# Down projection of a hybrid decoder layer: a second buffer of results for the first chunk, and the second sums scaled and added at the fifth product

## The chip, the cores and the metric

The kernel runs on one core of one Trainium2 chip. The metric is the time of one execution in device microseconds (us); shorter is better. The engines are named as the profile names them: PE (matmuls; PEld its weight loads), DVE (vector), ACT (scalar), POOL (GpSimd) and SP. SP and POOL issue nearly all transfers here.

## The reference

A decoder layer over 512 tokens and 16 meta tokens, width 2048: normalisation, one input projection, stick-breaking attention beside a gated short convolution, an output projection, and a SwiGLU feed-forward of width 5632. Only its last step is touched:

```python
n2 = _rmsnorm(h, g_ffn[l])
h = h + (jax.nn.silu(n2 @ w_gate[l]) * (n2 @ w_up[l])) @ w_down[l]
return h[:, N_META:]
```

The kernel holds everything transposed, as 16 output tiles of 128 features by 512 tokens. The normalisation's factor `r` is one number for each token, so it can be multiplied in after the product.

## The kernel before

**Numbers.** A float32 operand is split into a high part (`hi`, a cast, ACT, line 189) and a remainder (`lo`, a subtraction, DVE, line 190). A product of two tiles is three matmuls: hi by hi, hi by the activations' low part, lo by hi (lines 732, 733, 734).

**A pair of tiles by seven products.** `pair_product` computes two output tiles over two halves of the tokens as a 2x2 block product with Strassen's scheme in Winograd's form: seven block products instead of eight. In the down stage they run in the order x, z, x, z, x, y, x (first to seventh product), where x, y and z are PSUM banks with two buffers each. Seven sums of the activations, slots 0 to 6, are the moving operands. In between stand the evacuations: after the first product ACT copies x (p1, line 758), after the second z (p5, line 760), after the third x (u2, line 762); DVE forms `c2[:, 0]` after the fourth (line 764), `c2[:, 1]` after the fifth (line 768) and `c1[:, 0]` after the sixth (line 771); `c1[:, 1]` comes from the last x. So `c2` holds the "second sums", complete after the fifth product, and `c1` the "first sums", complete after the seventh. The fourth product adds onto z and so waits until line 760 has read it; the seventh adds onto x and waits for line 768.

**Chunks.** The inner dimension of the down projection, 22 blocks a half, goes in four chunks of 4, 6, 6 and 6 (`CHUNKS`). The first chunk is done with four output tiles at a time (`m=2`): 4 groups of seven products, each of 24 matmuls. They are called groups 0 to 3 here (`j` in the code). The other chunks have 8 pairs of two tiles each, seven products of 18 matmuls a pair.

**Results.** All sums lie in one buffer `d` of 4 x 512 numbers a partition. In the first chunk a group uses all of it: `c1` is `d[:, 0:2]`, `c2` is `d[:, 2:4]`, and since `sides` has no room for two tiles there, p5 is written to `c2[:, 1]` and u2 to `c2[:, 0]` by lines 760 and 762. In the later chunks pairs use the halves of `d` in turn. `scaled_sums` multiplies by r (`r_h`; line 1074 for c2, 1078 and 1079 for c1) and sends each tile to the output by a DMA that adds to what is there (`add_down`, line 1068, issued by POOL; "add" below).

**Loads.** Weights come by SP into `w_buf` as buffers get free. The activations of the chunk after come by POOL into ring places (`load_acts`, line 1040, two DMAs a slot, one each for the high and the low part; line 1033 is a small write that ties a load to the group before). The places of slots 5 and 6 of the second chunk are free only in group 3: slot 6's when the first three tiles of the pool `first` have been read. The names `fd1_6` and `ring1` in the rows below are slot 6 of the second chunk and its place.

**Order.** A scheduler places the instructions on the engines by its own estimates; each engine then runs its list in that order, and each waits only on semaphores. POOL's DMAs count on eight semaphores in turn (DMASW0 to 7).

Of the kernel before, what the change touches and what calls it, by code (L numbers as in the profile page):

```python
# [9 lines left out]
F32 = mybir.dt.float32  # L10
# [5 lines left out]
P = 128  # L16
D = 2048
SEQ = 512
# [8 lines left out]
T2 = SEQ // 2  # L27
# [6 lines left out]
def hybrid_layer(ctx: ExitStack, tc: tile.TileContext, xT, w_in, w_out, w_gu, w_down, vecs, out):  # L34
# [12 lines left out]
    def open_pool(name, bufs=1, **kw):  # L47
        return tc.alloc_tile_pool(name=name, bufs=bufs, reuse_waits="tile", **kw)
# [13 lines left out]
    def t512(cols=SEQ, tag="t", bufs=6):  # L62
        n_tmp[0] += 1
        pool = atmp if tag == "r" else tmp
        return pool.tile([P, cols], F32, tag=tag, bufs=bufs, name=f"tmp{n_tmp[0]}")
# [371 lines left out]
    def two(t):  # L437
        return t.rearrange("p (a b) -> p a b", a=2)
# [225 lines left out]
    def halves_of(cols):  # L664
        return t512(2 * CH, cols, 2)[:, : 2 * CH]

    for j in range(CONV_FIRST):
        if j == 0:
            after(2, lambda: form_blocks(7))
        c1, c2 = halves_of("e"), halves_of("e2")  # L670
# [45 lines left out]
    sides = cpool.tile([P, 3 * CH], F32, name="sides_c")  # L716
# [3 lines left out]
    def block_product(ps, act, start, m=1):  # L720

        hi, lo, n = next_w()
        w, n = ps.shape[-1] // m, n // m
        for j in range(m):
            p, skip = ps[:, j * w : (j + 1) * w], m > 1 or not start
            for k in range(n):  # L730
                kk = slice((j * n + k) * P, (j * n + k + 1) * P)
                pe.matmul(p, hi[:, kk], act(0, k), start=start and j == k == 0, stop=False, skip_group_check=skip)  # L732
                pe.matmul(p, hi[:, kk], act(1, k), start=False, stop=False, skip_group_check=skip)  # L733
                pe.matmul(p, lo[:, kk], act(0, k), start=False, stop=k == n - 1, skip_group_check=skip)  # L734

    def pair_product(acts, c1, c2, sides, m=1, fourth=None):

        i, cols = ents[used[0]][0], c1.shape[-1]
        w, first = cols // m, pairs[i][1]

        def bank(name):
            return xyz.tile([P, 512], F32, tag=name, name=f"{name}{i}")[:, :cols]

        def side(name):
            n = {"p1": 0, "p5": 1, "u2": 2}[name]
            if m == 1 or not n:
                return sides[:, n * w : n * w + cols]  # L750
            return c2[:, 2 - n]

        y, z, x = bank("y"), bank("z"), bank("x")
        p1, p5, u2 = side("p1"), side("p5"), side("u2")
        if first:
            block_product(y, acts[5], True, m)
        block_product(x, acts[0], True, m)
        sc.copy(p1, x)
        block_product(z, acts[1], True, m)
        sc.copy(p5, z)  # L760
        block_product(x, acts[2], False, m)
        sc.copy(u2, x)
        block_product(z, acts[3], False, m)
        ve.scalar_tensor_tensor(c2[:, 0], z, -1.0, u2, ALU.mult, ALU.subtract)
        if fourth:
            fourth()
        block_product(x, acts[4], False, m)
        ve.scalar_tensor_tensor(c2[:, 1], x, -1.0, p5, ALU.mult, ALU.subtract)  # L768
        if not first:
            block_product(y, acts[5], True, m)  # L770
        ve.tensor_tensor(c1[:, 0], y, p1, ALU.add)
        block_product(x, acts[6], False, m)
        return x

    def pair(acts):
        c1, c2 = halves_of("e"), halves_of("e2")
        x = pair_product(acts, two(c1), two(c2), sides)
        sc.copy(two(c1)[:, 1], x)
        return c1, c2

    for j in range(CONV_FIRST, HEADS, 2):
        ys = []
        for m in range(2):
            c1, c2 = pair(conv_acts)
# [16 lines left out]
        for m in range(2):  # L801
            s = t512(SEQ, "e", 2)[:, :SEQ] if j == HEADS - 2 else cpool.tile([P, SEQ], F32, tag="s", name=f"sq{j}_{m}")
# [45 lines left out]
    def pad(pool, n):  # L848
        pool.tile([P, n // 4], F32, name=f"pad_{pool.name}")

    acts = {}
# [33 lines left out]
    for i, j in enumerate(OUT_TILES):  # L885
# [32 lines left out]
        if i == KT - 1:  # L918
# [9 lines left out]
            sides = fp.tile([P, 3 * T2], F32, name="sides")  # L928
            rings_p = {0: open_pool("ring_0")}
            pad(rings_p[0], 32)  # L930
            rings, n_ring, ring = {}, [7], {}
# [3 lines left out]
            def new_places(i):  # L935
                p, m = groups[i]
                for n, t in enumerate(slots(rings_p[p], F32R, m, 6, f"ring{i}", tail=4 if i == 7 else 60, tag=f"ring{i}")):
                    ring[i + n] = t
# [31 lines left out]
    def act_of(t):  # L970
        return lambda part, k: t[:, part, k]
# [21 lines left out]
    at = [(c, k) for c, n in enumerate(CHUNKS) for k in range(n)]  # L993
# [32 lines left out]
    def load_acts(c, s, behind=None):  # L1026

        if c < len(CHUNKS):
            n = CHUNKS[c]
            if c:  # L1030
                rings[c, s] = ring_place()[:, :, :n]
                if behind is not None:
                    gp.tensor_scalar(rings[c, s][:, :, 0, 0], behind[:, :2], 1.0, 0.0, ALU.mult, ALU.add)
            elif s:
                rings[c, s] = slot(first, F32R, n, f"first{s}", f"first{s}")
            else:
                rings[c, s] = ring[0][:, :, :n]

            for part in range(2):
                gp.dma_start(rings[c, s][:, part], fd[c][s][:, part], max_dma_last_dim=3072)  # L1040

    for f in range(FT):
        g1 = apool.tile([P, 2, T2], F32, tag="c1", name=f"g{f}")
        u1 = apool.tile([P, 2, T2], F32, tag="c2", name=f"u{f}")
        x = pair_product(acts_of, g1, u1, sides, 1, None if f else h_scale)
# [7 lines left out]
    first = open_pool("ring_first", side="right")  # L1053
    with tc.high_priority(1 << 20):
        for s in range(1, 7):
            load_acts(0, s)
    pad(first, 11936)
    gate(FT - 1, g1, u1, x)
    apool.release()
    fpool_last.release()  # L1060
# [1 line left out]
    d = cpool.tile([P, 4, SEQ], F32, name="d")  # L1062
# [4 lines left out]
    def add_down(j, c):  # L1067
        gp.dma_start(two(out[j]), c, accum_op=ALU.add)  # L1068

    def scaled_sums(j, c1, c2, x, m):  # L1070

        for n in range(m):
            at = slice(n * T2, n * T2 + T2)
            ve.tensor_tensor(c2[:, :, at], c2[:, :, at], r_h, ALU.mult)  # L1074
            add_down(j + 2 * n + 1, c2[:, :, at])
        for n in range(m):
            at = slice(n * T2, n * T2 + T2)
            ve.tensor_tensor(c1[:, 0, at], c1[:, 0, at], r_h[:, 0], ALU.mult)
            ve.tensor_tensor(c1[:, 1, at], x[:, at], r_h[:, 1], ALU.mult)
            add_down(j + 2 * n, c1[:, :, at])  # L1080

    for j in range(KT // 4):
        for s in ((0, 1), (2, 3), (4,))[j - 1] if j else ():
            load_acts(1, s, last)
        c1, c2 = d[:, 0:2], d[:, 2:4]
        last = c2[:, 0]
        x = pair_product([act_of(rings[0, s]) for s in range(7)], c1, c2, sides, 2)
        if j == KT // 4 - 1:
            first.release()
            rings_p[1] = open_pool("ring_a", side="right")  # L1090
            for i in (1, 3, 4, 5):
                new_places(i)
            pad(rings_p[1], 160)
            for s in (5, 6):
                load_acts(1, s)
        scaled_sums(4 * j, c1, c2, x, 2)
    for c in range(1, len(CHUNKS)):
        end = c == len(CHUNKS) - 1
        for j in range(KT // 2):

            if 1 <= j <= 5:
                load_acts(c + 1, j - 1, last)
            c1, c2 = (two(d[:, j % 2 * 2 + m]) for m in range(2))
            last = c2[:, 0]
            last_pair = end and j == KT // 2 - 1
            if last_pair:
                h2 = slots(rings_p[1], F32, 1, 2, "h2", tag="ring4")[0].rearrange("p a k t -> p (a k) t")
                h2 = [h2[:, 2 * m : 2 * m + 2] for m in range(2)]
                for m in (1, 0):
                    nc.sync.dma_start(h2[m], two(out[2 * j + m]))  # L1110
            x = pair_product([act_of(rings[c, s]) for s in range(7)], c1, c2, sides)
            if j == KT // 2 - 1:
                for s in (5, 6):
                    load_acts(c + 1, s)
            if last_pair:
                ve.tensor_tensor(c2, c2, r_h, ALU.mult)
                ve.tensor_tensor(c2, c2, h2[1], ALU.add)
                nc.sync.dma_start(two(out[2 * j + 1]), c2)
                ve.tensor_tensor(c1[:, 0], c1[:, 0], r_h[:, 0], ALU.mult)
                ve.tensor_tensor(c1[:, 0], c1[:, 0], h2[0][:, 0], ALU.add)  # L1120
                ve.tensor_tensor(c1[:, 1], x, r_h[:, 1], ALU.mult)
                ve.tensor_tensor(c1[:, 1], c1[:, 1], h2[0][:, 1], ALU.add)
                nc.sync.dma_start(two(out[2 * j]), c1)
            else:
                scaled_sums(2 * j, c1, c2, x, 1)
    rings_p[2].release()
    cpool.release()
    rings_p[1].release()
# [59 lines left out]
```

## Time and profile before

| | us |
|---|---|
| median of 3 runs | 2090.63 (2089.04 to 2090.69) |
| the profiled execution | 2091.11 |
| its span, first to last instruction | 2087.8 |
| PE busy | 2046.0 (98%) |
| DVE busy | 1723.3 (83%) |
| ACT busy | 1046.5 (50%) |
| POOL busy | 414.9 (20%) |
| mean granted TensorE clock | 0.991 |

The times inside the trace are us from the span's start. A row of a timeline gives start and duration, engine, line, operation, output<-input, and in brackets how long the engine had waited and for whom. "PE busy" counts any time with a matmul under way; it does not say whether the matmuls follow each other at full pace. The down stage is the stretch from 1635.77 to the end.

### The profile page before, as it was taken

Reading aid. Unit: us, or ns where it says so; the run is one execution under the profiler, and the core shown is the slowest. Engines: PE = TensorE matmul, PEld = TensorE weight load, DVE = VectorE, ACT = ScalarE, POOL = GpSimd, SP = SyncE. Lnnn points to the kernel's source line nnn. Section 1 sums busy time; section 2 is a strip of 40 time slices with the busy share of each in tenths; the row PEclk is TensorE's granted clock in tenths of the full one; section 3 lists DMA queues with packets and bytes.
Section 4 is the critical chain, followed back from the end, with each engine's and each line's share of the span. In section 5 each row is a group of like instructions: output and inputs, shape, how many; then the busy total and the mean of one; then the engine's idle time right before and its main releaser. Section 6 shows DMA issues by size and latency. Waiting matters only on the chain.

```text
span 2087.8 us, 39731 instructions
## 1 busy us (share of the span) xinstructions
PE 2046.0 (98%) x16158; PEld 1979.0 (95%) x16158; DVE 1723.3 (83%) x2186; ACT 1046.5 (50%) x1511; POOL 414.9 (20%) x559
## 2 busy tenths in 40 slices
PE   8999999999999998999999999999999889999999
PEld 6999999999998888999999999999999889999999
DVE  7878877578877778998989989989899867888887
ACT  5666656444443435554555555545555433444443
POOL 3111111220015443111110111111101332223110
PEclk8999999999999999999999999999999989999999
DMA  6343334653356656556554555655555989989864
GB/s 205 107 152 118 121 123 133 219 154 106 103 205 186 183 177 217 153 175 175 163 162 149 169 154 148 173 155 162 164 150 172 300 239 237 262 233 252 242 155 86
DMA packets 161686, 362.21 MB, mean 173 GB/s; under 512 B 13456, under 2 KB 73360, under 8 KB 161504
## 3 DMA queue, kind: packets, MB, share of 16 engines
q1 hardware_dynamic: 78368, 225.80, 34.3%
q0 software_dynamic: 83136, 133.89, 24.4%
q8 instruction: 126, 2.06, 0.4%
q14 instruction: 56, 0.46, 0.1%
HBM read 278.76 MB, written 80.87 MB: 172 GB/s over the span
## 4 chain that ended last, share of the span: by engine, by line
PE 88%; DMA 3%; DVE 3%; issue 2%; ACT 1%; POOL 1%; SPq 0%; DVEq 0%; POOLq 0%; ACTq 0%
PE x L732 12%; PE x L734 12%; PE x L733 12%; PE z L732 6%; PE z L733 6%; PE z L734 6%; PE y L733 3%; PE y L732 3%; PE y L734 3%; PE po L829 3%; PE po L830 3%; PE po L831 3%; PE pv L276 1%; PE pv L278 1%; PE pv L280 1%
## 5 line engine op out<-in xcount | busy, mean ns | idle before, releaser
L189 ACT CAST s_buf<-w_buf 128x1024 fp32r<-128x1024 f32 (+2 forms) x665 | 659.4, 992 | 790.4 <-PE x L733 350.6
L190 DVE TENSOR_TENSOR s_buf<-w_buf,s_buf 128x1024 fp32r<-128x1024 f32 (+2 forms) x665 | 769.8, 1158 | 197.8 <-ACT s_buf L189 196.7
L733 PE MATMUL x<-f,s_buf 128*128 128x256 f32 x1408 | 388.3, 276 | 3.0 <-DMA f<-fx 1.8
L734 PE MATMUL x<-f,s_buf 128*128 128x256 f32 x1408 | 388.1, 276 | 3.0 <-DVE s_buf L190 3.0
L732 PE MATMUL x<-f,s_buf 128*128 128x256 f32 x1408 | 388.1, 276 | 0.2 <-ACT f L290 0.2
L198 DVE TENSOR_TENSOR w_buf<-w_buf 128x1024 f32<-128x1024 f32 (+1 forms) x243 | 278.5, 1146 | 19.0 <-DMA w_buf<-w_in 10.7
L733 PEld LDWEIGHTS x<-f,s_buf 128*128 128x128 f32 x1408 | 265.0, 188 | 3.4 <-DMA f<-fx 2.0
L734 PEld LDWEIGHTS x<-f,s_buf 128*128 128x128 f32 x1408 | 265.1, 188 | 3.2 <-DVE s_buf L190 3.2
L732 PEld LDWEIGHTS x<-f,s_buf 128*128 128x128 f32 x1408 | 265.0, 188 | 0.5 <-ACT f L290 0.4
L1002 POOL DMA_DIRECT2D fd<-s x147 | 103.9, 925 | 690.8 <-DVE s L291 689.2
L732 PE MATMUL z<-f,s_buf 128*128 128x256 f32 x704 | 193.6, 275 | 0.0
L733 PE MATMUL z<-f,s_buf 128*128 128x256 f32 x704 | 193.6, 275 | 0.0
L734 PE MATMUL z<-f,s_buf 128*128 128x256 f32 x704 | 193.6, 275 | 0.0
L732 PE MATMUL x<-ring,s_buf 128*128 128x256 f32 x608 | 168.1, 276 | 4.4 <-DVE d L768 4.4
L734 PE MATMUL x<-ring,s_buf 128*128 128x256 f32 x608 | 168.0, 276 | 1.0 <-DVE s_buf L190 1.0
L733 PE MATMUL x<-ring,s_buf 128*128 128x256 f32 x608 | 168.0, 276 | 0.0
L733 PEld LDWEIGHTS z<-f,s_buf 128*128 128x128 f32 x704 | 132.1, 188 | 0.1
L732 PEld LDWEIGHTS z<-f,s_buf 128*128 128x128 f32 x704 | 132.1, 188 | 0.0
L734 PEld LDWEIGHTS z<-f,s_buf 128*128 128x128 f32 x704 | 132.1, 188 | 0.0
L1068 POOL DMA_DIRECT2D out_T<-d x62 | 60.1, 990 | 326.6 <-DVE d L1074 273.8
L732 PEld LDWEIGHTS x<-ring,s_buf 128*128 128x128 f32 x608 | 114.8, 189 | 4.6 <-DVE d L768 4.6
L734 PEld LDWEIGHTS x<-ring,s_buf 128*128 128x128 f32 x608 | 114.9, 189 | 1.2 <-DVE s_buf L190 1.2
(380 smaller groups left out, 5310.2 us busy)
## 6 DMA issues: line engine op xcount, KB each, us to landing
w_buf<-w_gu SPq DMA_DIRECT2D x176, 512.0 KB, 3.4
w_buf<-w_in SPq DMA_DIRECT2D x92, 512.0 KB, 3.4
fd<-s POOLq DMA_DIRECT2D x147, 256.0 KB, 5.3
w_buf<-w_down SPq DMA_DIRECT2D x96, 384.0 KB, 4.9
ring<-fd POOLq DMA_DIRECT2D x42, 768.0 KB, 8.9
w_buf<-w_out SPq DMA_DIRECT2D x32, 512.0 KB, 3.5
out_T<-d POOLq DMA_DIRECT2D x62, 256.0 KB, 5.4
fc<-st SPq DMA_DIRECT2D x8, 1040.0 KB, 6.2
```

Of the source, the lines that this page charges most:

```text
L189: sc.copy(hi, src)
L190: ve.tensor_tensor(lo, src, hi.bitcast(F32), ALU.subtract)
L198: ve.tensor_tensor(sums[name], a, b, ALU.add)
L276: pe.matmul(ps, wh, ah[:, a:b], start=k == 0, stop=False)
L732: pe.matmul(p, hi[:, kk], act(0, k), start=start and j == k == 0, stop=False, skip_group_check=skip)
L733: pe.matmul(p, hi[:, kk], act(1, k), start=False, stop=False, skip_group_check=skip)
L734: pe.matmul(p, lo[:, kk], act(0, k), start=False, stop=k == n - 1, skip_group_check=skip)
L829: pe.matmul(ps, hi[:, kk], ah, start=k == order[0], stop=False)
L830: pe.matmul(ps, hi[:, kk], al, start=False, stop=False)
L831: pe.matmul(ps, lo[:, kk], ah, start=False, stop=k == order[-1])
L1002: gp.dma_start(fd[c][s][:, :, k], t[:, :, i])
L1068: gp.dma_start(two(out[j]), c, accum_op=ALU.add)
```

## The change

It has two parts. A second buffer `d2` of the same size is taken from the pool `first`, out of what was padding, and the first chunk's groups use `d` and `d2` in turn. And the work on the second sums (times r, add to the output) moves out of `scaled_sums` into `pair_product`, to a place behind line 768, as the function `second_sums`; `first_sums` keeps the rest. The very last pair is left as it was.

```diff
     def pair_product(...)
         block_product(x, acts[4], False, m)
         ve.scalar_tensor_tensor(c2[:, 1], x, -1.0, p5, ALU.mult, ALU.subtract)
+        if second:
+            second()
         if not first:
             block_product(y, acts[5], True, m)
...
-    pad(first, 11936)
+    d2 = first.tile([P, 4, SEQ], F32, name="d2")
+    pad(first, 11936 - 8192)
...
-    def scaled_sums(j, c1, c2, x, m):
-
-        for n in range(m):
-            at = slice(n * T2, n * T2 + T2)
+    def second_sums(j, c2, m):
+        for n, at in columns_of(m):
             ve.tensor_tensor(c2[:, :, at], c2[:, :, at], r_h, ALU.mult)
-            add_down(j + 2 * n + 1, c2[:, :, at])
+            add_down(j + n + 1, c2[:, :, at])
+    def first_sums(j, c1, x, m):
...
-        c1, c2 = d[:, 0:2], d[:, 2:4]
+        c1, c2 = (d, d2)[j % 2][:, 0:2], (d, d2)[j % 2][:, 2:4]
         last = c2[:, 0]
-        x = pair_product([act_of(rings[0, s]) for s in range(7)], c1, c2, sides, 2)
+        x = pair_product(
+            [act_of(rings[0, s]) for s in range(7)], c1, c2, sides, 2, None, lambda: second_sums(4 * j, c2, 2)
+        )
         if j == KT // 4 - 1:
             first.release()
...
             for s in (5, 6):
                 load_acts(1, s)
-        scaled_sums(4 * j, c1, c2, x, 2)
+        first_sums(4 * j, c1, x, 2)
```

The line numbers shift: 1068 becomes 1071 (the add), 1074 becomes 1079 (c2 times r), 1078 and 1079 become 1085 and 1086 (c1 times r), 771 becomes 773, 1033 and 1040 become 1035 and 1042.

What it moves lies in the first chunk and the first two pairs of the second; in the later chunks the scheduler had line 1074 behind line 768 already, and the lists are the same.

On ACT, in group 1 of the first chunk, there stood (`x54` and `z54` are that group's banks):

```order
L758 COPY sides_7920<-x54_17691 128x512 [waits DVE_49,PE_49]
L189 CAST s_buf_117<-w_buf_116 128x1024 [waits DVE_49,PE_49,Activation_49]
L760 COPY d_17468<-z54_17690 128x512 [waits DMASW7_49,DMASW1_49,PE_49]
L189 CAST s_buf_117<-w_buf_116 128x1024 [waits DMAHW2_49,DVE_49,PE_49]
L762 COPY d_17468<-x54_17691 128x512 [waits PE_49,Pool_49]
```

and now stands:

```order
L758 COPY sides_7920<-x54_17692 128x512 [waits DVE_49,PE_49]
L189 CAST s_buf_117<-w_buf_116 128x1024 [waits DVE_49,PE_49,Activation_49]
L760 COPY d2_17446<-z54_17691 128x512 [waits PE_49]
L189 CAST s_buf_117<-w_buf_116 128x1024 [waits DMAHW2_49,DVE_49,PE_49]
L762 COPY d2_17446<-x54_17692 128x512 [waits PE_49]
```

The copy of p5 no longer waits for the two adds of the group before (DMASW7 and DMASW1); in groups 2 and 3 it waits for those of two groups before.

On POOL, from the middle of group 2 to the end of group 3, there stood:

```order
L1040 DMA ring7_17473<-fd1_4_7965 128x2x768 [waits DMASW2_49]
L1068 DMA out_T<-d_17468 256x1x256 [waits DMASW3_49,DVE_49]
L1068 DMA out_T<-d_17468 256x1x256 [waits DMASW4_49,DVE_49]
L1040 DMA ring0_7925<-fd1_5_7966 128x2x768 [waits DMASW5_49,PE_49]
L1040 DMA ring0_7925<-fd1_5_7966 128x2x768 [waits DMASW6_49]
L1068 DMA out_T<-d_17468 256x1x256 [waits DMASW7_49,DVE_49]
L1040 DMA ring1_18321<-fd1_6_7967 128x2x768 [waits DMASW0_49,PE_49]
L1040 DMA ring1_18321<-fd1_6_7967 128x2x768 [waits DMASW1_49]
L1068 DMA out_T<-d_17468 256x1x256 [waits DMASW2_49,DVE_49]
L1068 DMA out_T<-d_17468 256x1x256 [waits DMASW3_49,DVE_49]
L1068 DMA out_T<-d_17468 256x1x256 [waits DMASW4_49,DVE_49]
```

and now stands:

```order
L1042 DMA ring7_17474<-fd1_4_7965 128x2x768 [waits DMASW2_49]
L1042 DMA ring0_7925<-fd1_5_7966 128x2x768 [waits DMASW3_49,PE_49]
L1071 DMA out_T<-d_17469 256x1x256 [waits DMASW4_49,DVE_49]
L1071 DMA out_T<-d_17469 256x1x256 [waits DMASW5_49,DVE_49]
L1042 DMA ring0_7925<-fd1_5_7966 128x2x768 [waits DMASW6_49]
L1071 DMA out_T<-d2_17446 256x1x256 [waits DMASW7_49,DVE_49]
L1071 DMA out_T<-d2_17446 256x1x256 [waits DMASW0_49,DVE_49]
L1071 DMA out_T<-d2_17446 256x1x256 [waits DMASW1_49,DVE_49]
L1071 DMA out_T<-d2_17446 256x1x256 [waits DMASW2_49,DVE_49]
L1042 DMA ring1_18326<-fd1_6_7967 128x2x768 [waits DMASW3_49,PE_49]
L1042 DMA ring1_18326<-fd1_6_7967 128x2x768 [waits DMASW4_49]
```

The two loads of slot 6 (`fd1_6`) stood behind the first of group 3's four adds; now they stand behind all four.

On PE, at the seventh product of the second chunk's first pair, which reads slot 6 (`x57` is its bank, `x58` that of the next pair's first product), there stood:

```order
L734 MATMUL y57_18340<-ring0_7925,s_buf_117 128x256
L732 MATMUL x57_18342<-ring1_18321,s_buf_117 128x256 [waits DMASW0_49,DVE_49]
L733 MATMUL x57_18342<-ring1_18321,s_buf_117 128x256 [waits DMASW1_49]
L734 MATMUL x57_18342<-ring1_18321,s_buf_117 128x256
L732 MATMUL x57_18342<-ring1_18321,s_buf_117 128x256
```

and now stands, after the first matmul of x57, which waits for slot 6's high part (DMASW3), and fourteen matmuls of x58:

```order
L734 MATMUL x58_18510<-ring7_17474,s_buf_117 128x256
L732 MATMUL x58_18510<-ring7_17474,s_buf_117 128x256
L733 MATMUL x58_18510<-ring7_17474,s_buf_117 128x256
L733 MATMUL x57_18343<-ring1_18326,s_buf_117 128x256 [waits DMASW4_49]
L734 MATMUL x57_18343<-ring1_18326,s_buf_117 128x256
```

So 17 matmuls of the next pair stand between the matmul that waits for the high part of slot 6 and the one that waits for its low part.

More of the change, by code (lines that the diff above doesn't have):

```diff
@@ L734, in block_product, with pair_product @@
                 pe.matmul(p, lo[:, kk], act(0, k), start=False, stop=k == n - 1, skip_group_check=skip)
-    def pair_product(acts, c1, c2, sides, m=1, fourth=None):
+    def pair_product(acts, c1, c2, sides, m=1, fourth=None, second=None):
         i, cols = ents[used[0]][0], c1.shape[-1]
@@ L1068, in add_down, with columns_of @@
         gp.dma_start(two(out[j]), c, accum_op=ALU.add)
-    def scaled_sums(j, c1, c2, x, m):
-        for n in range(m):
-            at = slice(n * T2, n * T2 + T2)
+    def columns_of(m):
+        return [(2 * n, slice(n * T2, n * T2 + T2)) for n in range(m)]
+    def second_sums(j, c2, m):
+        for n, at in columns_of(m):
             ve.tensor_tensor(c2[:, :, at], c2[:, :, at], r_h, ALU.mult)
-            add_down(j + 2 * n + 1, c2[:, :, at])
-        for n in range(m):
-            at = slice(n * T2, n * T2 + T2)
+            add_down(j + n + 1, c2[:, :, at])
+    def first_sums(j, c1, x, m):
+        for n, at in columns_of(m):
             ve.tensor_tensor(c1[:, 0, at], c1[:, 0, at], r_h[:, 0], ALU.mult)
             ve.tensor_tensor(c1[:, 1, at], x[:, at], r_h[:, 1], ALU.mult)
-            add_down(j + 2 * n, c1[:, :, at])
+            add_down(j + n, c1[:, :, at])
     for j in range(KT // 4):
@@ L1110, in hybrid_layer @@
                     nc.sync.dma_start(h2[m], two(out[2 * j + m]))
-            x = pair_product([act_of(rings[c, s]) for s in range(7)], c1, c2, sides)
+            x = pair_product(
+                [act_of(rings[c, s]) for s in range(7)], c1, c2, sides, 1, None,
+                None if last_pair else lambda: second_sums(2 * j, c2, 1),
+            )
             if j == KT // 2 - 1:
@@ L1124, in hybrid_layer @@
             else:
-                scaled_sums(2 * j, c1, c2, x, 1)
+                first_sums(2 * j, c1, x, 1)
     rings_p[2].release()
```

## The prediction

> **What bounds the kernel now.** I read the page first.
>
> ```profile
> span 2087.8 us, 39731 instructions
> PE 2046.0 (98%) x16158; PEld 1979.0 (95%) x16158; DVE 1723.3 (83%) x2186; ACT 1046.5 (50%) x1511; POOL 414.9 (20%) x559
> ```
>
> The matmuls fill the span, so a step matters only where PE waits for it or runs at a lower clock. Next, the view of waits, for the down stage alone (total us, count, longest).
>
> ```profile
> ACT d L760 <- DMA out_T<-d: 16.2, 3, 5.5
> PE z L732 <- ACT d L760: 13.0, 3, 4.4
> DVE d L764 <- DMA out_T<-d: 5.2, 1, 5.2
> PE x L732 <- DVE d L768: 4.7, 2, 4.4
> ```
>
> Three times ACT's copy of p5 waits for adds of the group before, which still read `d`, and three times PE's fourth product waits for that copy. Once DVE's line 764, in the second chunk's first pair, waits for an add, and PE's seventh product for line 768 behind it. Then PE's timeline.
>
> ```profile
> 1638.49 0.28 PE L732 MATMUL z<-first,s_buf 128*128 128x256 f32 x1
> 1641.21 0.28 PE L732 MATMUL x<-first,s_buf 128*128 128x256 f32 x1
> ...
> 1653.56 0.39 PE L734 MATMUL x<-ring,s_buf 128*128 128x256 f32 x1 [0.97 <-DVE s_buf L190]
> 1658.82 0.28 PE L732 MATMUL z<-first,s_buf 128*128 128x256 f32 x1
> 1668.79 0.58 PE L732 MATMUL z<-first,s_buf 128*128 128x256 f32 x1 [4.37 <-ACT d L760]
> 1673.87 0.28 PE L732 MATMUL x<-first,s_buf 128*128 128x256 f32 x1
> 1684.75 0.28 PE L732 MATMUL z<-first,s_buf 128*128 128x256 f32 x1
> 1711.40 0.28 PE L732 MATMUL z<-first,s_buf 128*128 128x256 f32 x1
> 1736.43 0.28 PE L732 MATMUL z<-ring,s_buf 128*128 128x256 f32 x1
> 1751.20 0.38 PE L732 MATMUL x<-ring,s_buf 128*128 128x256 f32 x1 [4.40 <-DVE d L768]
> 1757.03 0.28 PE L732 MATMUL z<-ring,s_buf 128*128 128x256 f32 x1
> 1771.31 0.28 PE L732 MATMUL z<-ring,s_buf 128*128 128x256 f32 x1
> ```
>
> The row at 1638.49 starts the second product of group 0, that at 1641.21 its third: 24 matmuls took 2.72 us, .1133 each. So a product of the first chunk costs 2.72 us and a group seven of them, 19.04. In the second chunk a product has 18 matmuls, 2.04 us, and a pair 14.28; the last two rows are 14.28 apart. The five other z rows begin the second products of groups 1 to 3 and of the second chunk's first two pairs. The fourth product of group 1 (1668.79) took 5.08 us instead of 2.72 after its wait; the last view, by windows (busy time, then clock, DMA share and GB/s), says why.
>
> ```profile
> 1620.90:1640.00 19.10, 19.10 (x171) 19.10 (x170) 15.98 (x19) 9.55 (x14) 7.61 (x11) 1.00 1.07 321
> 1640.00:1656.10 16.10, 15.13 (x133) 14.94 (x132) 15.75 (x19) 8.04 (x10) 1.40 (x2) 1.00 1.05 342
> 1656.10:1682.00 25.90, 21.53 (x170) 21.33 (x169) 16.29 (x19) 8.84 (x10) 9.58 (x9) 0.87 0.95 247
> 1668.79:1673.87 5.08, 5.08 (x25) 5.08 (x26) 1.22 (x1) 1.38 (x2) 0.00 (x0) 0.53 1.19 314
> 1682.00:1708.70 26.70, 22.28 (x171) 22.08 (x170) 17.59 (x22) 8.83 (x10) 8.88 (x10) 0.87 0.86 236
> 1708.70:1734.40 25.70, 21.23 (x171) 20.87 (x170) 17.41 (x23) 9.24 (x11) 10.31 (x12) 0.93 0.95 257
> ```
>
> The granted clock was 0.53 in that product: a wait of 4.4 us is paid a second time as matmuls at half pace.
>
> **The second buffer, in groups 1 to 3.** With `d` and `d2` in turn, line 760 waits for nothing in group 1, and in groups 2 and 3 for adds of two groups before. In group 2 those are group 0's, issued about a group (19 us) earlier; adds took 8.5 to 8.9 us to land (row below), so the wait goes. What PE wins is the distance between second products over 19.04: 1684.75 − 1658.82 = 25.93 gives 6.89; 1711.40 − 1684.75 = 26.65 gives 7.61; for group 3, 25.03 against six products of 2.72 and one of 2.04, 18.36, gives 6.67. Group 0's 20.33 holds no such wait: its 1.29 stays (.97 of it line 190). Group 3's may keep 0.3 of DVE lateness at line 768, which I leave in. Sum: 21.2 − 0.3 = 20.9.
>
> **The same in the second chunk's first pair.** `d` was last group 2's now, so line 764 finds it free, and line 768 comes in time: 1757.03 − 1736.43 = 20.60 against 14.28 gives 6.32. Gains together: 27.2 us.
>
> Of this 17.4 are the waits themselves (13.0 + 4.4), the rest is half clock. Another short wait shows that this second price has a threshold here:
>
> ```profile
> 806.69 0.38 PE L733 MATMUL x<-f,s_buf 128*128 128x256 f32 x1 [1.76 <-DMA f<-fx]
> 812.78 0.38 PE L734 MATMUL x<-f,s_buf 128*128 128x256 f32 x1 [2.96 <-DVE s_buf L190]
> 807.00:809.00 2.00, 2.00 (x20) 2.00 (x19) 0.00 (x0) 0.49 (x1) 1.35 (x2) 1.00 1.13 418
> 814.00:816.00 2.00, 2.00 (x11) 2.00 (x11) 1.97 (x2) 0.00 (x0) 0.00 (x0) 0.50 0.62 234
> ```
>
> After 1.76 us the clock stayed 1.00, after 2.96 it was 0.50. [...]
>
> **The second sums at the fifth product.** The instructions are the same in number and size: two multiplications by r in a group, two adds of c2, two of c1. They stand ahead of line 773 now instead of behind it, which makes line 773 later by at most one 0.69-us operation against a free next product; nothing on PE waits for it but the next evacuation of x. I take 0 in groups 0 to 3; the cover is DVE's room, 17.4 to 17.6 us of work for a group of 19.04. If it failed, DVE's lateness would cost the price of the second rival. In chunks two to four DVE's list is the same: 0.
>
> **The loads of slot 6, moved behind all adds of group 3.** This is the one new wait I expect. POOL before:
>
> ```profile
> 1738.13 1.12 POOL L1068 DMA_DIRECT2D out_T<-d  x1 [3.12 <-DVE d L1074]
> 1739.66 2.26 POOL L1068 DMA_DIRECT2D out_T<-d  x2 [0.41 <-DVE d L1079]
> ...
> L1068 POOL DMA_DIRECT2D out_T<-d x2: 1087/1098/1108, 1739.7 to 1740.8; - x2
> DMA to landing us min/median/max: 8.5/8.7/8.9
> ...
> L1040 POOL DMA_DIRECT2D ring<-fd x2: 1203/1208/1213, 1733.1 to 1733.8; - x2
> DMA to landing us min/median/max: 6.3/8.0/9.7
> ...
> L1040 POOL DMA_DIRECT2D ring<-fd x42: 737/772/2347, 1659.4 to 1960.4; - x42
> DMA to landing us min/median/max: 5.8/8.9/16.6
> ```
>
> The end of group 3 is E = 1736.43 − 2.04 = 1734.39. The loads of slot 6 went ahead of it, at 1733.1 and 1733.8, and landed 6.3 and 9.7 us later, 1739.4 and 1743.5: before the seventh product at 1751.20. The last adds went at 1739.66 and 1740.8, E + 5.3 and E + 6.4; they hang on DVE's work after line 768, which is the same in number. So the loads now go at about E + 7.1 and E + 7.8 (the queue's spacing in the rows above). Without other waits the seventh product starts at E + 6 x 2.04 = E + 12.24, 5.1 us after the first load's issue; the shortest of 42 loads took 5.8. So PE waits, by 0.7 to 11.5 us as the ends of that row have it (16.6 − 5.1). I take 7.9: the 6.3 of the same load, and about 1.6 for two adds (256 KB each) just ahead of it in the queue. The high and low parts (768 KB each) landed 1743.5 − 1739.4 = 4.1 us apart, so 512 KB are 2.7, of which some 1.1 us have passed while the adds are issued ahead. PE waits 2.8 us for the high part. The low part lands 4.1 later; 17 matmuls of the next pair (17 x .1133 = 1.9 at full pace) fill a part, and about 2.0 more is lost, as a wait or as half clock that fills it. Together +4.8, between 0.7 and 13.5 (11.5 + 2.0); a gain is excluded, since no matmul waited for slot 6 before.
>
> [...]
>
> **The sum.** 2091.11 (the profiled execution: span 2087.8 and 3.3 around it) − 27.2 + 4.8 = 2068.7. The median of the runs, 2090.63, lies 0.48 below that execution: 2068.2.
>
> **Rivals.**
>
> *No new wait at slot 6.* The loads go earlier than E + 7, since POOL is free before, or land in under 5 us. Then −27.5 − 0.48: 2063.1. For it: DVE's end after line 768 could come sooner with ACT no longer stalled. Against: no load under 5.8.
>
> *The DMA engines or DVE become the bound of the first chunk.* The groups would come in 19 us instead of 25 to 27, and move in that time what they move now. A group moves 247 GB/s x 25.90 = 6.40 MB, in 19.04 us 336 GB/s; the stretches at full clock moved 321 and 342 with a share of 1.05 to 1.07, so there is no room left above it. If weights come late, line 190 does, and PE with it, as in group 0 (1.29 us a group). Three groups so: +3.9, 2072. Its far end: groups as long as 20.33 plus one wait of 3 us and its half clock each (about 5 us, as between the 812.78 row and the clock's return), 2068.2 + 15 = 2083. Against: group 0 and the stretch ahead ran at full clock at that very rate.
>
> *Slower.* Slot 6, or a weight ahead of it, lands so late that the gain is eaten. The load would have to take 5.1 + 27 = 32 us from its issue, double the longest row, 16.6. Or each of the 28 products of the first chunk waits 1 us for its weights: the stage's weight loads landed within 11.9 us at most,
>
> ```profile
> DMA to landing us min/median/max: 2.9/4.9/11.9
> ```
>
> and would have to be later than the products they are issued ahead. From 28 x 1.0 = 28 us on it decides the sign; then 2091 and more.
>
> *No effect.* The adds of two groups before could still be under way, or the first wait be replaced by one of equal length at the same product (z's release by line 764): the waits stay, 2090.6. Against: 19 us of distance against 8.9 of landing.
>
> **How the numbers follow.** Forecast with the new wait (2064 to 2072): 0.59. No new wait (2062.5 to 2064): 0.15. DMA or DVE bound (2071 to 2083): 0.20. No effect: 0.03. Slower: 0.03. About 0.2%, 4.2 us, is what a measurement of this kernel can tell from no change. The first three cases all gain more than that: faster 0.59 + 0.15 + 0.20 = 0.94, same 0.03, slower 0.03. The low end is all the gain and no new wait, 2063.1 less 0.6 for the runs' own spread; the high end takes slot 6's load at 14 us (2091.11 − 27.2 − 0.48 + (14 − 5.1) + 2.0 = 2074.3) and the milder half of the DMA case: 2074.5. Left out are the other half of it, no effect and slower, 0.16.
>
> **What would show it.** Right: no wait of ACT's line 760 or DVE's line 764 for an add; second products of groups 1 to 3 19.0 to 20.4 us apart; clock 1.00 from 1660 to the end of group 3; one wait of 2 to 4 us at the seventh product of the second chunk's first pair, for the DMA into the ring, with a short stretch of half clock. Wrong: that wait over 8 us or missing, waits of PE for line 190 in every group, a fourth product that still waits for line 760.

## The result: 2070.75 us, and where the time went

| | us |
|---|---|
| before, median of 4 runs | 2090.66 (2089.04 to 2091.67) |
| after, median of 4 runs | 2070.75 (2066.04 to 2071.88) |
| ratio | 0.9887, 95% interval 0.9862 to 0.9912 |
| forecast | 2068.2, range 2062.5 to 2074.5 |
| the profiled execution after | 2071.88, span 2069.7 |

The page of the kernel after, the two lines that answer to those shown of before:

```profile
span 2069.7 us, 39728 instructions
PE 2038.4 (98%) x16158; PEld 1972.2 (95%) x16158; DVE 1724.3 (83%) x2186; ACT 1046.4 (51%) x1511; POOL 412.3 (20%) x559
```

Its shares for PE and DVE are those of before, 98% and 83%, and do not tell the two kernels apart; the waits of the down stage do. These are all of PE's:

```profile
PE x L732 <- DVE d L1085: 3.9, 1, 3.9
PE x L734 <- DVE s_buf L190: 0.7, 1, 0.7
PE x L732 <- DVE d L768: 0.3, 1, 0.3
```

The three waits for line 760 (13.0 us) and the 4.4-us wait for line 768 are gone, and one wait of 3.9 us is new. PE's timeline at the same products as before (the second products of groups 0 to 3 and of the second chunk's first two pairs, and the new wait), then the windows between them:

```profile
1640.58 0.28 PE L732 MATMUL z<-first,s_buf 128*128 128x256 f32 x1
1660.62 0.28 PE L732 MATMUL z<-first,s_buf 128*128 128x256 f32 x1
1679.66 0.28 PE L732 MATMUL z<-first,s_buf 128*128 128x256 f32 x1
1698.70 0.28 PE L732 MATMUL z<-first,s_buf 128*128 128x256 f32 x1
1717.62 0.28 PE L732 MATMUL z<-ring,s_buf 128*128 128x256 f32 x1
1731.92 0.77 PE L732 MATMUL x<-ring,s_buf 128*128 128x256 f32 x2 [3.93 <-DVE d L1085]
1738.95 0.28 PE L732 MATMUL z<-ring,s_buf 128*128 128x256 f32 x1
```

```profile
1640.58:1660.62 20.04, 19.34 (x170) 19.15 (x169) 19.45 (x23) 10.51 (x12) 4.38 (x4) 1.00 1.07 329
1660.62:1679.66 19.04, 19.04 (x170) 19.04 (x169) 16.33 (x19) 8.83 (x10) 9.19 (x14) 1.00 1.12 319
1679.66:1698.70 19.04, 19.04 (x170) 19.04 (x169) 17.18 (x21) 8.84 (x10) 8.59 (x11) 1.00 1.14 327
1698.70:1717.62 18.92, 18.64 (x164) 18.48 (x163) 17.03 (x23) 9.02 (x11) 6.89 (x8) 1.00 1.13 331
1717.62:1738.95 21.33, 17.40 (x129) 17.23 (x128) 13.38 (x21) 6.81 (x11) 6.67 (x8) 0.84 1.10 313
```

Groups 1 and 2 now take 19.04 us, the bare time of 168 matmuls, at clock 1.00; group 3 takes 18.92 against 18.36. The second chunk's first pair takes 21.33 against 14.28, at clock 0.84. The row at 1731.92 is put down to DVE's line 1085, which that matmul does not wait for; of its two semaphores, slot 6's load and line 768, the load came last. POOL's timeline, then the issues of that load by its line, with the time to landing:

```profile
1720.70 2.19 POOL L1071 DMA_DIRECT2D out_T<-d  x2 [4.53 <-DVE d L1086]
1722.37 2.01 POOL L1042 DMA_DIRECT2D ring<-fd  x2
```

```profile
L1042 POOL DMA_DIRECT2D ring<-fd x2: 1269/1276/1282, 1722.4 to 1723.1; - x2
DMA to landing us min/median/max: 9.4/10.6/11.9
```

1722.37 + 9.4 = 1731.8, and PE starts at 1731.92.

The stretch from group 0's second product to that of the second chunk's second pair, called **the stretch** below, took 1757.03 − 1638.49 = 118.54 before and 1738.95 − 1640.58 = 98.37 after: 20.2 less. The whole execution gained 2091.11 − 2071.88 = 19.2; the first chunk began 2.1 later in this execution (group 0's second product at 1640.58, not 1638.49), and the time around the span was 1.1 shorter (2.2, not 3.3). Behind the stretch both traces agree to 0.02 us. The two traced executions of the changed kernel, this one and the one below, are each the slowest of their four runs, so the stretch of the others may be shorter; no trace shows theirs.

### The profile page after: what moved, and what is told of

Same layout as the page of the kernel before. It is cut to its first block, busy times and chain, and to the rows that moved or that the text cites. A ratio compares the mean times of both kernels' runs of the same rounds, so it can differ in the third digit from the quotient of the medians.

```text
span 2069.7 us, 39728 instructions
## 1 busy us (share of the span) xinstructions
PE 2038.4 (98%) x16158; PEld 1972.2 (95%) x16158; DVE 1724.3 (83%) x2186; ACT 1046.4 (51%) x1511; POOL 412.3 (20%) x559
## 4 chain that ended last, share of the span: by engine, by line
PE 92%; DVE 3%; DMA 1%; ACT 1%; issue 1%; POOL 0%; SPq 0%; DVEq 0%; ACTq 0%; POOLq 0%
PE x L732 13%; PE x L734 13%; PE x L733 13%; PE z L732 6%; PE z L733 6%; PE z L734 6%; PE y L733 3%; PE y L732 3%; PE y L734 3%; PE po L831 3%; PE po L833 3%; PE po L832 3%; PE pv L276 1%; PE pv L278 1%; PE pv L280 1%; PE pk L278 1%
## 5 line engine op out<-in xcount | busy, mean ns | idle before, releaser
L198 DVE TENSOR_TENSOR w_buf<-w_buf 128x1024 f32<-128x1024 f32 (+1 forms) x243 | 278.6, 1146 | 18.9 <-DMA w_buf<-w_in 10.1
```

The lines of the kernel that those rows point to most:

```text
L198: ve.tensor_tensor(sums[name], a, b, ALU.add)
```

## The experiments

Runs of the changed kernel differ by up to 6 us, those of the kernel before by up to 12, and the traces reach the first chunk up to 3.7 us apart, though all kernels run the same list up to there (last section). So each experiment is read by its stretch in the trace as well as by its time. The last three rows belong to a second series of runs, with runs of the kernel before of their own, to which their ratios refer. E is the end of group 3, 2.04 us ahead of the second product of the second chunk's first pair.

| kernel | median us (range) | ratio to before, 95% | stretch us | groups 0 to 3 | first pair |
|---|---|---|---|---|---|
| before | 2091.09 (2085.25 to 2097.21); second series 2093.30 (2086.77 to 2095.25) | | 118.54 | 20.33, 25.93, 26.65, 25.03 | 20.60 |
| after, again | 2067.80 (2067.28 to 2070.72) | 0.9892 (0.9874 to 0.9911) | 97.32 | 20.05, 19.04, 19.04, 18.92 | 20.27 |
| first part alone | 2073.82 (2070.51 to 2074.63) | 0.9916 (0.9901 to 0.9931) | 101.72 | 20.04, 19.04, 19.04, 18.91 | 24.69 |
| second part alone | 2078.31 (2075.34 to 2081.03) | 0.9938 (0.9920 to 0.9955) | 111.19 | 21.01, 19.04, 25.60, 23.95 | 21.59 |
| buffers and halves exchanged | 2065.78 (2064.70 to 2069.09) | 0.9883 (0.9864 to 0.9901) | 93.09 | 20.37, 19.04, 19.04, 18.92 | 15.72 |
| buffers exchanged | 2072.29 (2071.67 to 2076.04) | 0.9905 (0.9886 to 0.9924) | 100.60 | 20.06, 19.04, 19.04, 18.91 | 23.55 |
| small adds | 2065.03, one run | | 93.84 | 20.04, 19.04, 19.04, 18.91 | 16.81 |
| second part, tied to c1 | 2075.04 (2072.99 to 2076.02) | 0.9913 (0.9898 to 0.9928) | 101.25 | 20.47, 19.04, 19.65, 20.93 | 21.16 |

**The changed kernel again.** No edit.

> The changed kernel once more, as the measure for the others of this call. Theory (the waits for adds are gone, one wait for slot 6 is new): 2066 to 2072 us; second products of groups 1 to 3 19.0 us apart, one wait of 3 to 5 us at the seventh product of the second chunk's first pair, whose two second products are 20 to 22 us apart instead of 14.28. Rival (the part of the 1.9-us spread that the profiled execution showed ahead of the down stage is no accident but belongs to the change): the stretch ahead of the first chunk is again about 2 us longer than in the kernel before.

```profile
1731.95 0.47 PE L732 MATMUL x<-ring,s_buf 128*128 128x256 f32 x2 [4.07 <-DMA ring<-fd]
1737.78 0.28 PE L732 MATMUL z<-ring,s_buf 128*128 128x256 f32 x1
```

PE's timeline: the wait came again, 4.07 us, and here the trace names the load. As the rival has it, the first chunk began late again (group 0's second product at 1640.46).

**First part alone.** The second sums are multiplied and added after the seventh product.

```diff
-        x = pair_product([...], c1, c2, sides, 2, None, lambda: second_sums(4 * j, c2, 2))
+        x = pair_product([...], c1, c2, sides, 2)
...
+        second_sums(4 * j, c2, 2)
         first_sums(4 * j, c1, x, 2)
```

> First part alone: d and d2 in turn in the first chunk, the second sums of a group times r and added after the seventh product as before. Theory (the second buffer carries the whole gain, and the move of the second sums is worth nothing beside it): the time of the changed kernel within 2 us; groups 19.0 apart, the loads of slot 6 again behind all four adds and a wait of 3 to 6 us for them. Rival (the early add is a part of the gain): slower than the changed kernel by 4 us or more, with waits of PE for line 760 or for line 768 left.

My theory fell here: the move of the second sums is worth 101.72 − 97.32 = 4.4 us beside the second buffer, or 3.4 against the first trace of the changed kernel. But it is not a wait for line 760 that it saves, as the rival thought; the groups take 19.04 without it. POOL's timeline, slot 6's landing, and PE's timeline at its wait, in this run:

```profile
1695.98 4.56 POOL L1035 TENSOR_SCALAR ring<-d 128x2 fp32r<-128x2 f32 x1
1700.85 0.75 POOL L1042 DMA_DIRECT2D ring<-fd  x1 [0.30 <-POOL ring L1035]
...
1720.84 2.01 POOL L1042 DMA_DIRECT2D ring<-fd  x2
```

```profile
L1042 POOL DMA_DIRECT2D ring<-fd x2: 1272/1280/1289, 1720.8 to 1721.6; - x2
DMA to landing us min/median/max: 13.3/13.9/14.5
```

```profile
1734.25 0.77 PE L732 MATMUL x<-ring,s_buf 128*128 128x256 f32 x2 [7.94 <-DMA ring<-fd]
```

The loads of slot 6 go as early as in the changed kernel, E + 6.9 against E + 6.8, and behind the same four adds, but the first lands 13.3 us after its issue instead of 9.4 and 9.6. What is late is the queue ahead of those adds. Slot 5's last load, by its line, in the first trace of the changed kernel and then in this run (the later of the two issues):

```profile
L1042 POOL DMA_DIRECT2D ring<-fd x1: 1733/1733/1733, 1704.1 to 1704.1; - x1
DMA to landing us min/median/max: 15.8/15.8/15.8
```

```profile
L1042 POOL DMA_DIRECT2D ring<-fd x2: 2328/2337/2346, 1704.2 to 1704.9; - x2
DMA to landing us min/median/max: 16.7/17.8/18.9
```

It landed at 1704.1 + 15.8 = 1719.9, E + 4.3, there, and at 1704.9 + 18.9 = 1723.8, E + 9.9, here. From slot 4's first load to slot 6's, POOL's transfers landed in the order of their issue in both traces, each 1.3 to 4.0 us behind the one ahead, so a late start of this queue is made good only in part. Slot 4's first load (1700.85) went at E − 13.1 here and at E − 18.6 in the changed kernel. Of these 5.5 us, 3.7 are line 1035's small write, which took 4.56 us instead of 0.83, and the rest is the add of c2 ahead of it, which goes later; 4.0 us of them are left when slot 6 lands. Why the write took longer is not shown.

**Second part alone.** One buffer d.

```diff
-        c1, c2 = (d, d2)[j % 2][:, 0:2], (d, d2)[j % 2][:, 2:4]
+        c1, c2 = d[:, 0:2], d[:, 2:4]
```

> Second part alone: one buffer d, the second sums times r and added at the fifth product. Theory (an add of c2 leaves about 0.5 us ahead of the group's end instead of 3.7 behind it and lands in 8 to 9.5, so line 760 is late by about 1.3 us a group, too little for half clock; the second chunk's first pair keeps its wait for the add of c1, 6.3 us with the half clock, and slot 6 is not late): 2091 - (20.9 - 3 x 1.3) = 2074 us, between 2070 and 2080. Rival 1 (when an add lands is set by the transfers' traffic, not by when it goes): 2088 to 2092, waits of 3 to 4 us left. Rival 2 (the move alone takes the waits wholly): 2069 to 2070.

PE's timeline at the fourth products of groups 2 and 3, and POOL's between groups 1 and 2:

```profile
1686.05 0.58 PE L732 MATMUL z<-first,s_buf 128*128 128x256 f32 x1 [3.51 <-ACT d L760]
1711.35 0.39 PE L732 MATMUL z<-first,s_buf 128*128 128x256 f32 x1 [3.22 <-ACT d L760]
```

```profile
1674.15 1.94 POOL L1035 TENSOR_SCALAR ring<-d 128x2 fp32r<-128x2 f32 x2
1675.25 1.51 POOL L1042 DMA_DIRECT2D ring<-fd  x1
1676.02 1.91 POOL L1071 DMA_DIRECT2D out_T<-d  x1
```

2078.31 lies in the expected range, but the waits are not as expected: none in group 1, over 3 us in groups 2 and 3. POOL's rows show why. Group 1 ends at 1676.93 − 2.72 = 1674.21. The second add of c2 goes 1.8 behind that instead of 0.5 ahead, since line 1035's two small writes and a load stand before it in POOL's list. In the second chunk's first pair the wait for line 768 stays, 4.58 us.

**Second part alone, with the loads tied to c1.** One word more.

```diff
-        last = c2[:, 0]
+        last = c1[:, 0]
```

> The second part alone (one buffer d), and the small write of line 1035 that ties a slot's load to the group before now reads c1 instead of c2, so that no load stands between a group's two adds of c2 in POOL's queue. Theory (in the run of the second part alone the second add went 1.5 to 1.8 us behind the group's end instead of 0.5 ahead, held up by that write and a load; it lands 8 to 9.4 later and line 760 waits for it): the waits of 3.5 and 3.2 us at line 760 shrink to 0.3 to 1.5, without half clock, so groups 2 and 3 take 19.3 to 20.5 us instead of 25.6 and 23.95; 100 to 104 us from the second product of group 0 to that of the second chunk's second pair, instead of 111.2. Rival (an add lands when the traffic lets it): waits over 2.5 us, 108 us or more.

PE's timeline at its three waits:

```profile
1684.05 0.39 PE L732 MATMUL z<-first,s_buf 128*128 128x256 f32 x1 [0.29 <-ACT d L760]
1705.12 0.39 PE L732 MATMUL z<-first,s_buf 128*128 128x256 f32 x1 [1.71 <-ACT d L760]
1733.43 0.58 PE L732 MATMUL x<-ring,s_buf 128*128 128x256 f32 x1 [4.33 <-DVE d L768]
```

With nothing between a group's two adds, the waits of 3.51 and 3.22 us fall to 0.29 and 1.71, and the stretch to 101.25, in the expected range (1.71 and group 3's 20.93 a little over theirs). So the wait for an add follows the add's place in POOL's list. Most of what d2 brings in the groups can be had without it: groups 1 to 3 take 59.6 us here, 77.6 before and 57.0 in the changed kernel.

**Buffers and halves exchanged.** d2 lies in the pool `first`, out of which slot 6's place comes. Here group 3 uses `d`, and the second chunk's pairs start with the half that held c2.

```diff
-        c1, c2 = (d, d2)[j % 2][:, 0:2], (d, d2)[j % 2][:, 2:4]
+        c1, c2 = (d2, d)[j % 2][:, 0:2], (d2, d)[j % 2][:, 2:4]
...
-            c1, c2 = (two(d[:, j % 2 * 2 + m]) for m in range(2))
+            c1, c2 = (two(d[:, (j + 1) % 2 * 2 + m]) for m in range(2))
```

> The changed kernel with d2 for groups 0 and 2 and d for groups 1 and 3, so that d2, which lies in the pool whose release frees slot 6's place, is not used by group 3; and the second chunk's pairs begin with the half of d that held c2. The loads of slot 6 then stand behind two adds instead of four. Theory (their place in POOL's queue makes them late): they go about 0.5 us behind group 3's end, 11.7 ahead of their use, so the wait is gone or under 1 us: 2063 us, 5 to 8 below the changed kernel. Rival (transfers are slow there because the DMA engines are full, wherever the loads stand): the wait moves to a weight or to line 764 and the time stays within 2 us of the changed kernel.

Slot 6's loads by POOL's timeline and by their line, and PE's timeline at its wait:

```profile
1713.82 1.99 POOL L1042 DMA_DIRECT2D ring<-fd  x2
```

```profile
L1042 POOL DMA_DIRECT2D ring<-fd x2: 1250/1256/1263, 1713.8 to 1714.5; - x2
DMA to landing us min/median/max: 10.9/11.8/12.8
```

```profile
1727.39 0.38 PE L733 MATMUL x<-ring,s_buf 128*128 128x256 f32 x1 [1.14 <-DMA ring<-fd]
```

The loads go at E + 0.1, with two adds ahead of them, not four, and land no sooner after their issue than in the changed kernel (10.9 and 12.8). What counts is the place in the queue, two adds further ahead: the first lands at E + 11.0 instead of E + 16.2. PE waits 1.14 us for the low part, and the stretch is 93.09, 4.2 and 5.3 below the two traces of the changed kernel. It is the best version here by its trace; by the times, where 5 to 8 us less were expected, it can't be told from the changed kernel (2065.78 and 2067.80, and the intervals overlap).

**Buffers exchanged alone.** The same without the second line of the diff.

> As the version with exchanged buffers and halves, but the second chunk's pairs begin with the half of d that held c1, as in the kernel before. Theory (the 6.3 us of the second chunk's first pair hang on line 764 finding its half of d still under an add): the adds of c1 go at about 5.1 and 6.2 us behind group 3's end and land near 14, line 764 needs the place at 8.2; the seventh product waits 3.5 to 4.5 us for line 768 and half clock follows: the pair's second products 20 to 21.6 apart, 97 to 99.5 us from the second product of group 0 to that of the second chunk's second pair (93.1 with the halves exchanged, 97.3 in the changed kernel). Rival (the wait in that pair was slot 6 all along): 93 to 94 us, since slot 6's loads stand behind two adds here too.

DVE's wait in the view of waits, group 3's adds of c1 by their line, and PE's timeline:

```profile
DVE d L764 <- DMA out_T<-d: 6.9, 1, 6.9
```

```profile
L1071 POOL DMA_DIRECT2D out_T<-d x2: 1104/1113/1122, 1719.4 to 1720.5; - x2
...
DMA to landing us min/median/max: 10.7/10.8/10.9
```

```profile
1732.75 0.58 PE L732 MATMUL x<-ring,s_buf 128*128 128x256 f32 x1 [6.13 <-DVE d L768]
```

The wait of the kernel before is back, though both parts of slot 6 had landed by 1728.8, 4.0 us before the wait ended: it hung on line 764 and the half of `d`, not on slot 6. It is larger than expected, 6.13 us instead of 3.5 to 4.5, because the adds land 10.7 to 10.9 us after their issue, not 8.5 to 8.9. 1.5 MB of slot 6 now go 5 us ahead of them in the same queue, and the first of the adds landed 1.3 us behind the last of it.

**Small adds.** The two adds of c1 of group 3 send 16 of 128 partitions; the rest of those two tiles is not added.

```diff
-    def add_down(j, c):
-        gp.dma_start(two(out[j]), c, accum_op=ALU.add)
+    def add_down(j, c, rows=P):
+        gp.dma_start(two(out[j])[:rows], c[:rows], accum_op=ALU.add)
...
-            add_down(j + n, c1[:, :, at])
+            add_down(j + n, c1[:, :, at], 16 if m == 2 and j == KT - 4 else P)
```

> The changed kernel, in which the two adds of c1 of group 3, right ahead of slot 6's loads in POOL's queue, send only 16 of 128 partitions (32 KB instead of 256 KB each); the rest of those two tiles is left out of the output. Number and place of the transfers are the same. Theory (the bytes just ahead of a load in its queue are what makes it land in 9.5 us instead of 6.3): the load lands 6 to 7.5 us after its issue, PE's wait is 0.3 to 2 us, and no half clock follows; the pair's second products 14.6 to 16.5 apart. Rival (a load of 768 KB takes that long because the weights and loads as a whole fill the DMA engines): landing 9 to 10, wait 3.5 to 4.5, 20 to 21.5 apart.

Slot 6's loads by POOL's timeline and by their line, and PE's timeline at its waits:

```profile
1718.90 1.99 POOL L1042 DMA_DIRECT2D ring<-fd  x2
```

```profile
DMA to landing us min/median/max: 7.0/8.3/9.6
```

```profile
1726.04 0.47 PE L732 MATMUL x<-ring,s_buf 128*128 128x256 f32 x2 [1.03 <-DMA ring<-fd]
1729.26 0.39 PE L733 MATMUL x<-ring,s_buf 128*128 128x256 f32 x1 [0.91 <-DMA ring<-fd]
```

The load lands in 7.0 us instead of 9.6, and PE's wait falls from 4.07 to 1.03 and 0.91; 0.5 us of that is the earlier issue (E + 6.3 against E + 6.8). The bytes of the adds just ahead make the load late; 448 KB less of them are 2.6 us. In the queue, the two small adds had landed 1.1 us after the adds of c2 ahead of them, the full ones 3.7 us after. The pair's 16.81 is 0.2 over the expected range.

## Why the prediction was right, point by point

**The waits that go.** Right. Groups 1 to 3 gained 6.89 + 7.61 + (25.03 − 18.92) = 20.6 us, where 20.9 was forecast, after the 0.3 that I left in group 3; line 768 kept 0.28 there. Lines 760 and 764 wait for no add any more. The landing of 8.5 to 8.9 us that stands behind this was read from two late adds; others of the kernel before took up to 14.7 (issued at 1662.86), still less than the 19 us between groups. The loss in the second chunk's first pair was line 764's: with that wait gone and 1.14 us of slot 6's left the pair takes 15.72 (halves exchanged), with line 764's wait back 23.55 (buffers exchanged).

**The new wait.** Right in place and cause, too small in size: 4.8 was forecast; the pair lost 21.33 − 14.28 = 7.05 us in the profiled execution and 5.99 in the other. Three terms: the issue came at E + 6.8 (E + 7.1 forecast); the high part landed 9.4 us later, not 7.9; and the half clock behind the wait cost 7.05 − 3.93 = 3.1, and 1.9 in the other execution, where 2.0 stood. The step that was mis-sized is "some 1.1 us have passed": I priced the two adds by a load's rate, 2.7 us for 512 KB, and took off what moves during the issue. The runs put the delay that the two adds leave at 2.6 us for 448 KB. And more was under way than the two: when the load went at 1722.37, the second add of c2 and both adds of c1 had yet to land, which they did 2.1, 3.5 and 5.7 us later, and the load followed 3.7 us behind the last. In the kernel before, one add was ahead of the same load; it landed 3.3 us after the load's issue and the load 3.0 behind it, which is the 6.3 that the sum started from. The low part brought no wait of its own; the 17 matmuls of the next pair, at half pace, covered it.

**The second sums cost 0.** The cover held: DVE had 16.3 to 17.2 us of work in 19.04, and line 773 held up nothing on PE (ACT's line 758 once, by 0.4 us). That they also gain, 3.4 to 4.4 us, I had not seen; that gain was inside the forecast's number only because the order of the changed kernel was read as it is.

**The sum.** In the profiled execution the stretch gained 20.2 instead of 27.2 − 4.8 = 22.4, the other time 21.2. The medians, 2070.75 and 2067.80, lie around the forecast of 2068.2; their difference is of the size of the spread.

**The rivals.** No new wait: not so, 3.93 us. DMA engines or DVE as the bound: not so; groups 1 to 3 ran at clock 1.00 with a DMA share of 1.12 to 1.14 at 319 to 331 GB/s, above group 0's 1.07, and no wait for line 190. So there was room above the share of 1.05 to 1.07 that the prediction held to be full. No effect, slower: not so.

## What to carry to other kernels

A second buffer takes away a wait, but see what its memory was lent from: here it made a load that comes out of the same pool go behind four adds, and about a quarter of the 27 us was paid back. Price a transfer by its place in its issuer's list and by everything ahead of it that has yet to land, not by its own size alone: here an add of 256 KB landed 1.3 to 3.2 us behind the transfer ahead of it in the changed kernel's traces. Count a wait together with the slow stretch behind it, where one follows: here 3.1 us were lost at half clock behind a wait of 3.93.

## What the runs showed of the hardware

**In these traces the loss at half clock did not follow the length of the wait.** Behind waits of 3.93 to 7.94 us in the second chunk's first pair, the next 36 matmuls, 4.08 us at full pace, took between 5.83 (wait 4.07: 1737.78 − 1731.95) and 7.06 us (wait 6.13): 1.8 to 3.0 us lost, 2.3 behind the longest (1740.63 − 1734.25 = 6.38 in the first part alone). In the changed kernel alone it was 3.0 in the first trace and 1.8 in the second. The stretches at half clock in the down stage of the kernel before, and those between them (busy times, then clock, DMA share and GB/s):

```profile
1666.78:1673.61 6.83, 4.82 (x22) 4.82 (x23) 1.22 (x1) 2.02 (x3) 0.00 (x0) 0.50 1.18 339
1673.61:1694.09 20.48, 16.74 (x148) 16.54 (x146) 15.95 (x19) 6.82 (x7) 8.88 (x10) 1.00 0.82 229
1694.09:1700.91 6.82, 6.14 (x28) 6.14 (x29) 1.78 (x2) 2.85 (x4) 0.00 (x0) 0.50 1.18 320
1700.91:1721.39 20.48, 16.27 (x142) 16.07 (x142) 15.49 (x19) 6.80 (x9) 8.35 (x9) 1.00 0.76 202
1721.39:1724.81 3.42, 3.42 (x17) 3.42 (x18) 1.23 (x1) 1.21 (x2) 0.00 (x0) 0.50 1.13 320
1724.81:1752.11 27.30, 22.64 (x196) 22.28 (x195) 19.98 (x28) 10.25 (x14) 5.88 (x6) 1.00 0.93 248
1752.11:1755.53 3.42, 3.42 (x18) 3.42 (x17) 3.42 (x6) 0.84 (x1) 2.32 (x4) 0.50 0.46 62
```

All seven last 3.41 us or 2, 6 or 8 times that, to 0.01. The one stretch at half clock in the down stage of the changed kernel, in its first trace and then in its second:

```profile
1731.14:1737.96 6.82, 6.04 (x28) 6.07 (x29) 0.67 (x2) 0.84 (x1) 0.99 (x2) 0.50 1.14 368
```

```profile
1732.75:1736.15 3.40, 3.40 (x19) 3.40 (x18) 0.00 (x0) 0.61 (x1) 0.00 (x0) 0.50 1.14 344
```

In the first, 6.0 us of it lay behind the wait's end at 1731.92, and 3.0 were lost; in the second all 3.4 lay behind the wait's end at 1731.95, and 1.8 were lost: about half of it both times. After waits of 1.71 us and less in the down stage the matmuls kept their pace (behind the 1.71, in the run tied to c1, the clock was 1.00 from 1705.10 to 1709.00).

**Of two waits of nearly one length, one had half clock behind it.** In the run of the second part alone PE waited 2.31 us up to 805.69 and 2.37 up to 811.20, ahead of the down stage. Its trace in windows of 3.41 us, laid from the start of the stretch at half clock, with PE's busy time first:

```profile
801.06:804.47 3.41, 2.32 (x20) 2.06 (x18) 3.12 (x3) 1.53 (x3) 1.27 (x2) 1.00 1.07 397
804.48:807.88 3.40, 2.19 (x19) 2.19 (x20) 0.13 (x1) 1.26 (x2) 1.78 (x2) 1.00 1.11 410
807.89:811.30 3.41, 1.04 (x10) 0.84 (x8) 2.93 (x3) 1.04 (x1) 3.24 (x3) 1.00 0.62 215
811.31:814.71 3.40, 3.40 (x17) 3.40 (x18) 3.27 (x4) 0.00 (x0) 0.96 (x1) 0.50 0.43 154
```

The first wait is spread over two windows, which are idle for 1.1 and 1.2 us, and the clock stayed 1.00. The second lies in one window, idle for 2.4 of its 3.4 us, and the next window had 0.50. The two waits that the prediction set side by side, 1.76 and 2.96 us, are 1.2 apart; these two differ by 0.06, so here the length of the wait does not tell. In windows laid in the same way over the down stages of the kernel before and of the changed kernel's first trace, the five ahead of a stretch at half clock were idle for 2.36 to 3.42 us. Of the windows at full clock with full clock behind them, the idlest was idle for 1.91. First the four of the kernel before with, as the last row, its 1.91, then the one of the changed kernel:

```profile
1663.37:1666.78 3.41, 1.05 (x10) 0.85 (x8) 0.61 (x1) 0.00 (x0) 2.46 (x3) 1.00 1.07 257
1690.67:1694.09 3.42, 0.00 (x0) 0.00 (x0) 0.00 (x0) 0.00 (x0) 1.89 (x3) 1.00 1.16 324
1717.98:1721.39 3.41, 0.18 (x1) 0.18 (x2) 0.00 (x0) 0.81 (x2) 0.97 (x2) 1.00 1.13 361
1748.70:1752.11 3.41, 0.91 (x7) 0.91 (x8) 3.41 (x6) 0.83 (x1) 0.00 (x0) 1.00 0.31 83
1745.29:1748.70 3.41, 1.50 (x14) 1.31 (x12) 0.05 (x1) 0.27 (x1) 0.00 (x0) 1.00 0.99 201
```

```profile
1727.72:1731.14 3.42, 0.27 (x3) 0.07 (x1) 3.42 (x6) 0.83 (x1) 1.99 (x3) 1.00 1.12 398
```

What sets the clock is not shown by this. One stretch at half pace, in the run of the first part alone, began at 796.80 (matmuls 0.21 us apart, 0.12 ahead of it) behind waits of only 0.22 and 1.26 us; its cause stays open.

**Where the runs differ.** Ahead of the first chunk all these kernels run the same list, and yet group 0's second product stood between 1636.88 and 1640.58 in the nine traces. A part arises early, and a part near 812, where PE waited 2.4 us (second part alone) to 6.2 us (the changed kernel) for line 190 at the start of the feed-forward part. Both traces of the changed kernel lie at the late end, all others earlier; whether that is the change or chance was not settled.
